# Split weights written at 32 different word offsets in their buffers, in a two-layer hybrid decoder trunk

## The chip, the cores and the metric

One core of one Trainium2 chip runs one program. The metric is the device time of one execution in microseconds; the kernel before was timed at 1593.85 us, the median of two runs (1593.66 and 1594.04).

## The reference

The kernel computes a small decoder trunk in float32: 256 tokens of width 1024 pass through two layers, each with a half-step SwiGLU feed-forward (width 2816), a mixing sub-layer with two branches (a Mamba-2 state-space branch and a gated DeltaNet branch on the same normalised input), and a second feed-forward; a last RMS norm closes it.

```python
for l in range(DEPTH):
    h = h + 0.5 * swiglu(rms_norm(h, ffn1_norm[l]), ffn1_w_in[l], ffn1_w_out[l])
    u = rms_norm(h, mix_norm[l])
    (z_s, xbc, dt_s, qkv, z_d, b_d, a_d, gate_s, gate_d) = jnp.split(u @ w_in[l], split_points, axis=-1)
    y_s = mamba2_branch(z_s, xbc, dt_s, ...)
    y_d = deltanet_branch(qkv, z_d, b_d, a_d, ...)
    merged = (jax.nn.sigmoid(gate_s) * (y_s @ ssm_w_branch[l])
              + jax.nn.sigmoid(gate_d) * (y_d @ dn_w_branch[l]))
    h = h + merged @ w_out[l]
    h = h + 0.5 * swiglu(rms_norm(h, ffn2_norm[l]), ffn2_w_in[l], ffn2_w_out[l])
return rms_norm(h, final_norm)
```

Nearly all of the arithmetic is in the products with the large weight matrices: w_in and w_out of the four feed-forwards, w_in of the mixer, the two branch projections and the mixer's w_out.

## The kernel before

The weights are laid out on the host, by pure reordering, as one stream of units of 128 x 2048 float32, in the order in which the kernel consumes them. A unit is used in two halves of 128 x 1024 words; there are 504 half units in all, numbered j.

Each half unit passes three stations. `load(j)` (line 93) issues a DMA on SyncE's queue into one of five `wraw` buffers. `prep(j)` (line 98) splits it: ScalarE copies the raw weights into `whi`, whose type is float32r and so rounds them, and VectorE subtracts, `wlo = wraw - whi`. `whi` and `wlo` have five buffers each. `take()` (line 111) hands the pair to the next consumer; each call also runs the loads and the splits ahead, so that up to five pairs stand ready and four more raw halves are on their way. Before the change every `whi` and `wlo` buffer is a tile of 128 x 1024 and is written from its first word.

The activations are split in the same way into a high and a low part. A product is then three float32r matmuls that add into one PSUM bank: high by high, and the two cross terms. Two helpers issue them: `mm3` (lines 208 to 211) with the weights as the streamed operand, 512 columns at a time, and the activations as the stationary one; `mm3w` (lines 213 to 216) with 128 columns of the weights as the stationary operand and 256 tokens of `uTh` or `uTl` streamed.

Three routines consume the half units. `tok_chunk` (line 218) is for outputs with tokens on the partitions: four half units, `mm3`, stationary `uTh` and `uTl`; its results are the tiles named f and t. `chan_chunk` (line 235) is for outputs with channels on the partitions: two half units, `mm3w`; its results are fc in the feed-forwards, and kk, qq, vv, zd, bc and xs in the mixer. `out_chunks` (line 254) is for the down projections: one half unit per 128 input channels, `mm3`, stationary `gh` and `gl` in the feed-forwards, `bh` and `bl` in the branch projections, `mh` and `ml` in the mixer's output; its results are named o and b. One further product, psm, uses `mm3w` with a small weight tile of 48 columns (`wsh`, `wsl`) that is split separately.

In a profile, a matmul is printed as output, then the streamed tile, then the stationary one: "fc<-uTh,whi" streams uTh against stationary whi, and "o<-whi,gh" streams whi against stationary gh. TensorE's weight loads stand in rows of their own under PEld.

The order of instructions on each engine follows the program, with a few pieces moved up by priority or held back behind a named instruction; the mixer's steps follow a list written out by hand (`ORDER`, lines 38 to 42). The tiles are placed in the on-chip memory by pools in the order of their creation: `h`, the constants, `uTh` and `uTl` and the norm weights first, then the five `wraw`, the five `whi` and the five `wlo` buffers, and behind them the large slots (`gh`, `gl` and the mixer's tiles), the 512-word scratch tiles (`bh`, `bl` and others) and the small ones. In the program as built, all five `whi` and all five `wlo` buffers lie 4096 bytes apart and begin on a multiple of 64 bytes within the partition; `uTh` and `uTl` begin 32 bytes past such a multiple; `gh`, `gl`, `bh`, `bl`, `mh`, `ml`, `wsh` and `wsl` on one.

Of the kernel before, what the change touches and what calls it, by code (L numbers as in the profile page):

```python
# [8 lines left out]
F32R = mybir.dt.float32r  # L9
I32 = mybir.dt.int32  # L10
AF = mybir.ActivationFunctionType
ALU = mybir.AluOpType
# [4 lines left out]
P = 128  # L17
# [12 lines left out]
NRAW = 5  # L30
NSPL = 5
START = 2

# [10 lines left out]
def trunk_kernel(ctx, tc, x, wst, wsm, norms, lpar, rpar, cst, out):  # L46
# [4 lines left out]
    wpool = ctx.enter_context(tc.tile_pool(name="wpool", bufs=1))  # L51
# [7 lines left out]
    def act(o, i, func=AF.Copy, **kw):  # L59
        return A.activation(out=o, in_=i, func=func, **kw)  # L60

    def tt(o, a, b, op):
        return V.tensor_tensor(out=o, in0=a, in1=b, op=op)  # L63
# [9 lines left out]
    def f(ap):  # L73
        return ap.bitcast(F32)
# [22 lines left out]

    def prep(j):
        r = raws.pop(j)
        hi = wpool.tile([P, 1024], F32R, tag="whi", name="whi", bufs=NSPL)  # L100
        lo = wpool.tile([P, 1024], F32R, tag="wlo", name="wlo", bufs=NSPL)
        act(hi[:], r[:])
        tt(lo[:], r[:], f(hi[:]), ALU.subtract)
        halves[j] = (hi, lo)

    def ahead(key, n, fn):
        while state[key] < min(n, n_halves):
            fn(state[key])
            state[key] += 1

    def take():
        j = state["taken"]
        state["taken"] = j + 1
        ahead("loaded", j + NSPL + NRAW - 1, load)
        ahead("prepped", j + 1 if state["hold"] else j + NSPL, prep)
        return halves.pop(j)
# [46 lines left out]
    def rstd_of(t):  # L163

        ss = small([P, 2], "ss")
        for n in range(2):
            junk = tmp2("junk")
            act(junk[:], h[:, t, n * 512 : (n + 1) * 512], AF.Square, scale=1.0 / 32.0, accum_out=ss[:, n : n + 1])
        z = small([P, 2], "zz")
        ts(z[:, 0:1], ss[:, 0:1], ss[:, 1:2], ALU.add, EPS, ALU.add)  # L170
        rsqrt(z[:, 1:2], z[:, 0:1], [P, 1])
        return z[:, 1:2]
# [18 lines left out]
    def norm_in(nw, add=None):  # L191

        for t in range(2):
            with tc.high_priority(offset=PRI):
                if add:
                    add(t)
                ins, done = rms_chain(t, nw)
            if t == 0:
                state["hold"] = False
                n = state["taken"]  # L200
                if not add:
                    ahead("prepped", n + 1, prep)
                    with tc.issue_after(done[0].ins), tc.issue_after(done[1].ins):
                        ahead("prepped", n + START, prep)
                with tc.issue_after(ins.ins):
                    ahead("prepped", n + 2, prep)
# [813 lines left out]
    for t in range(2):  # L1020
# [5 lines left out]
        r = rstd_of(t)  # L1026
# [123 lines left out]
```

## Time and profile before

| | us |
|---|---|
| Median of the two timed runs | 1593.85 |
| The profiled execution, its own time | 1593.43 |
| Span of its trace, first to last instruction | 1591.6 |
| DMA of one raw half unit (512 KB), issue to landing | 4.3 |
| ScalarE waiting before whi, all causes | 429.3 |
| VectorE waiting before wlo, all causes | 376.4 |

The mean granted TensorE clock is 0.999 of full speed over the span. A row of the profile's groups gives a line of the kernel, the engine, the operation and its tiles, then the total busy time, the mean of one instruction in nanoseconds, and the idle time of the engine just before. In rows of instructions in order of time, the first number is the start and the second the duration, both in microseconds. Matmuls overlap: each row's duration runs from entry to the modelled end of its pipeline, so that consecutive rows cover each other, and the pace of TensorE is the distance from start to start.

### The profile page before, as it was taken

What the parts mean: (1) busy time and instruction counts of PE and PEld (TensorE: products, weight loads), DVE (VectorE), ACT (ScalarE), POOL (GpSimd) and SP (SyncE); (2) the same over time, 40 slices, a digit from 0 to 9 for tenths busy, and PEclk for the clock granted to TensorE, in tenths of its full rate; (3) what the DMA queues carried; (4) which work ended last, traced back from release to release, by engine and by line L of the source; (5) the groups of instructions that cost most, each with busy time, mean ns of one, the idle gap of its engine ahead of it and who ended that gap; (6) DMA issues with size and microseconds to landing.
All of it is one profiled execution on the core that took longest, in us unless ns stands there. A gap on an engine that the chain in (4) does not pass through costs nothing.

```text
span 1591.6 us, 28859 instructions
## 1 busy us (share of the span) xinstructions
PE 1572.3 (99%) x11672; PEld 1420.9 (89%) x11672; DVE 1069.1 (67%) x1550; ACT 880.1 (55%) x1416; POOL 58.1 (4%) x60
## 2 busy tenths in 40 slices
PE   8999999999999999999999999999999999999998
PEld 7999879999888888999899987899998888889986
DVE  5555468957899766555465555698579996675554
ACT  5444468756565654444354444686656665454443
POOL 0000020000000000000000001000000000000000
PEclk9999999999999999999999999999999999999999
DMA  7555465543465456555565565655436555555562
GB/s 268 193 188 195 161 203 192 166 149 117 173 214 172 159 170 189 188 192 190 173 207 190 186 196 174 197 176 180 129 120 207 178 170 175 172 175 194 187 196 96
DMA packets 91915, 284.73 MB, mean 179 GB/s; under 512 B 22069, under 2 KB 23045, under 8 KB 90758
## 3 DMA queue, kind: packets, MB, share of 16 engines
q1 hardware_dynamic: 91782, 282.90, 54.8%
q8 instruction: 91, 1.49, 0.4%
q14 instruction: 42, 0.34, 0.1%
HBM read 280.94 MB, written 1.92 MB: 178 GB/s over the span
## 4 chain that ended last, share of the span: by engine, by line
PE 91%; DVE 4%; DMA 2%; ACT 1%; POOL 1%; issue 0%; SPq 0%; POOLq 0%; ACTq 0%
PE fc L216 9%; PE fc L214 9%; PE fc L215 9%; PE o L211 6%; PE o L209 5%; PE o L210 5%; PE t L209 4%; PE t L210 3%; PE t L211 3%; PE b L211 3%; PE b L210 2%; PE b L209 2%; PE xs L215 2%; PE xs L214 2%; PE xs L216 2%; DVE wlo L63 1%
## 5 line engine op out<-in xcount | busy, mean ns | idle before, releaser
L63 DVE TENSOR_TENSOR wlo<-wraw,whi 128x1024 fp32r<-128x1024 f32 x504 | 613.6, 1223 | 376.4 <-ACT whi L60 369.3
L60 ACT ACTIVATE whi<-wraw 128x1024 fp32r<-128x1024 f32 x504 | 531.0, 1060 | 429.3 <-PE fc L215 176.2
L214 PE MATMUL fc<-uTh,whi 128*128 128x256 f32 x1280 | 357.4, 279 | 0.0
L215 PE MATMUL fc<-uTl,whi 128*128 128x256 f32 x1280 | 357.0, 279 | 0.0
L216 PE MATMUL fc<-uTh,wlo 128*128 128x256 f32 x1280 | 357.0, 279 | 0.0
L215 PEld LDWEIGHTS fc<-uTl,whi 128*128 128x128 f32 x1280 | 240.6, 188 | 0.2
L214 PEld LDWEIGHTS fc<-uTh,whi 128*128 128x128 f32 x1280 | 240.6, 188 | 0.2
L216 PEld LDWEIGHTS fc<-uTh,wlo 128*128 128x128 f32 x1280 | 240.6, 188 | 0.0
L209 PE MATMUL o<-whi,gh 128*128 128x512 f32 x352 | 137.3, 390 | 0.0
L210 PE MATMUL o<-wlo,gh 128*128 128x512 f32 x352 | 137.3, 390 | 0.0
L211 PE MATMUL o<-whi,gl 128*128 128x512 f32 x352 | 137.0, 389 | 0.0
L209 PE MATMUL t<-whi,uTh 128*128 128x512 f32 x256 | 103.2, 404 | 1.0 <-ACT uTh L60 1.0
L210 PE MATMUL t<-wlo,uTh 128*128 128x512 f32 x256 | 101.6, 397 | 0.0
L211 PE MATMUL t<-whi,uTl 128*128 128x512 f32 x256 | 101.1, 396 | 0.0
L211 PEld LDWEIGHTS o<-whi,gl 128*128 128x128 f32 x352 | 66.1, 188 | 13.8
L210 PEld LDWEIGHTS o<-wlo,gh 128*128 128x128 f32 x352 | 66.1, 188 | 13.6
L209 PEld LDWEIGHTS o<-whi,gh 128*128 128x128 f32 x352 | 66.1, 188 | 13.4
L209 PE MATMUL b<-whi,bh 128*128 128x512 f32 x192 | 76.3, 399 | 0.0
L210 PE MATMUL b<-wlo,bh 128*128 128x512 f32 x192 | 74.9, 390 | 0.0
L211 PE MATMUL b<-whi,bl 128*128 128x512 f32 x192 | 74.3, 394 | 0.6 <-DVE bl L63 0.6
L214 PE MATMUL xs<-uTh,whi 128*128 128x256 f32 x256 | 73.1, 286 | 0.0
L216 PE MATMUL xs<-uTh,wlo 128*128 128x256 f32 x256 | 71.6, 280 | 0.0
(259 smaller groups left out, 2915.6 us busy)
## 6 DMA issues: line engine op xcount, KB each, us to landing
wraw<-in_wst_dram SPq DMA_DIRECT2D x504, 512.0 KB, 4.3
dc<-rdram SPq DMA_DIRECT2D x8, 1024.0 KB, 9.2
nw<-in_norms_dram SPq DMA_DIRECT2D x6, 512.0 KB, 4.9
gb<-rdram SPq DMA_DIRECT2D x8, 256.0 KB, 6.1
h<-in_x_dram SPq DMA_DIRECT2D x4, 256.0 KB, 3.1
out_dram<-fo SPq DMA_DIRECT2D x4, 256.0 KB, 2.3
dq<-X SPq DMA_DIRECT2D x2, 256.0 KB, 4.8
cs<-in_cst_dram SPq DMA_DIRECT2D x1, 384.0 KB, 8.2
```

Of the source, the lines that this page charges most:

```text
L60: return A.activation(out=o, in_=i, func=func, **kw)
L63: return V.tensor_tensor(out=o, in0=a, in1=b, op=op)
L209: PE.matmul(ps, lh, rh, start=start, stop=False)
L210: PE.matmul(ps, lh, rl, start=False, stop=False)
L211: PE.matmul(ps, ll, rh, start=False, stop=stop)
L214: PE.matmul(ps, wh, mh, start=start, stop=False)
L215: PE.matmul(ps, wh, ml, start=False, stop=False)
L216: PE.matmul(ps, wl, mh, start=False, stop=stop)
```

## The change

One constant is added and `prep` is changed. Every `whi` and `wlo` buffer gets 32 words per partition more, and half unit j is written at words j mod 32 to j mod 32 + 1023 of its buffer instead of 0 to 1023. The views of those 1,024 words are what `take()` hands out, so the consumers read the weights at the same offset. The raw buffers, the loads, the number and the order of instructions on every engine, and the arithmetic are as before. All tiles that are placed behind the buffers move up by 1,280 bytes (ten buffers, 128 bytes each).

```diff
 START = 2
+STEPS = 32
...
     def prep(j):
         r = raws.pop(j)
-        hi = wpool.tile([P, 1024], F32R, tag="whi", name="whi", bufs=NSPL)
-        lo = wpool.tile([P, 1024], F32R, tag="wlo", name="wlo", bufs=NSPL)
-        act(hi[:], r[:])
-        tt(lo[:], r[:], f(hi[:]), ALU.subtract)
+        at = slice(j % STEPS, j % STEPS + 1024)
+        hi = wpool.tile([P, 1024 + STEPS], F32R, tag="whi", name="whi", bufs=NSPL)[:, at]
+        lo = wpool.tile([P, 1024 + STEPS], F32R, tag="wlo", name="wlo", bufs=NSPL)[:, at]
+        act(hi, r[:])
+        tt(lo, r[:], f(hi), ALU.subtract)
         halves[j] = (hi, lo)
```

## The prediction

> **What bounds the kernel now.** I read the busy shares and the chain of waits first, then the groups of matmuls, then the starts of single matmuls in order of time.
>
> ```profile
> span 1591.6 us, 28859 instructions
> ...
> PE 1572.3 (99%) x11672; PEld 1420.9 (89%) x11672; DVE 1069.1 (67%) x1550; ACT 880.1 (55%) x1416; POOL 58.1 (4%) x60
> ...
> PE 91%; DVE 4%; DMA 2%; ACT 1%; POOL 1%; issue 0%; SPq 0%; POOLq 0%; ACTq 0%
> ...
> L63 DVE TENSOR_TENSOR wlo<-wraw,whi 128x1024 fp32r<-128x1024 f32 x504 | 613.6, 1223 | 376.4 <-ACT whi L60 369.3
> L60 ACT ACTIVATE whi<-wraw 128x1024 fp32r<-128x1024 f32 x504 | 531.0, 1060 | 429.3 <-PE fc L215 176.2
> ```
>
> TensorE is busy for 1572.3 of 1591.6 us and is 91% of the chain. The two instructions whose addresses change most directly, the rounding on ScalarE and the subtraction on VectorE, wait for others (429.3 and 376.4 us): they have room. So the time is the number of matmuls times the interval between their starts, and the question is whether that interval depends on where an operand begins.
>
> ```profile
> L214 PE MATMUL fc<-uTh,whi 128*128 128x256 f32 x1280 | 357.4, 279 | 0.0
> L214 PE MATMUL xs<-uTh,whi 128*128 128x256 f32 x256 | 73.1, 286 | 0.0
> L214 PE MATMUL zd<-uTh,whi 128*128 128x256 f32 x128 | 36.3, 284 | 0.0
> L214 PE MATMUL bc<-uTh,whi 128*128 128x256 f32 x128 | 36.3, 283 | 0.1
> L214 PE MATMUL qq<-uTh,whi 128*128 128x256 f32 x128 | 36.1, 282 | 0.0
> L214 PE MATMUL vv<-uTh,whi 128*128 128x256 f32 x128 | 35.9, 281 | 0.0
> L214 PE MATMUL kk<-uTh,whi 128*128 128x256 f32 x128 | 35.9, 281 | 0.0
> ...
> L209 PE MATMUL o<-whi,gh 128*128 128x512 f32 x352 | 137.3, 390 | 0.0
> L209 PE MATMUL t<-whi,uTh 128*128 128x512 f32 x256 | 103.2, 404 | 1.0 <-ACT uTh L60 1.0
> L209 PE MATMUL b<-whi,bh 128*128 128x512 f32 x192 | 76.3, 399 | 0.0
> L209 PE MATMUL f<-whi,uTh 128*128 128x512 f32 x64 | 26.5, 416 | 1.3 <-ACT uTh L60 1.3
> L209 PE MATMUL o<-whi,mh 128*128 128x512 f32 x64 | 25.1, 393 | 0.0
> ```
>
> Each of these rows stands for three (L214 to L216, or L209 to L211). The upper seven, 3 x (1280 + 256 + 5 x 128) = 6,528 matmuls, load the split weights as the stationary operand (named last) and stream 256 columns of uTh or uTl. The lower five, 3 x (352 + 256 + 192 + 64 + 64) = 2,784 matmuls, stream 512 columns of the split weights. The durations in these rows overlap, since matmuls are pipelined; what counts is start to start:
>
> ```profile
> 1529.72 0.39 PE L209 MATMUL o<-whi,gh 128*128 128x512 f32 x1
> ...
> 1543.32 0.39 PE L209 MATMUL o<-whi,gh 128*128 128x512 f32 x1
> ...
> 448.01 0.40 PE L209 MATMUL t<-whi,uTh 128*128 128x512 f32 x1
> ...
> 458.97 0.40 PE L211 MATMUL t<-whi,uTl 128*128 128x512 f32 x1
> ...
> 1499.85 0.28 PE L215 MATMUL fc<-uTl,whi 128*128 128x256 f32 x1
> ...
> 1511.75 0.28 PE L215 MATMUL fc<-uTl,whi 128*128 128x256 f32 x1
> ...
> 218.22 0.28 PE L214 MATMUL psm<-uTh,wsh 128*48 128x256 f32 x1
> ...
> 221.01 0.40 PE L209 MATMUL t<-whi,uTh 128*128 128x512 f32 x1
> ```
>
> These are the first and last of stretches without a gap: o 60 intervals in 13.60 us, 226.7 ns each; t 47 in 10.96, 233.2; fc 102 in 11.90, 116.7; psm 24 in 2.79, 116.3. The rows show that o and t, the same shape with the same streamed tile, differ by 6.5 ns, and twice 116.7 is 233.3. What differs by the program's own placement is the start of an operand: whi, wlo, gh, gl, wsh and wsl begin on multiples of 64 bytes in their partition, uTh and uTl 32 bytes (8 words) past one. Where no operand is off a 64-byte boundary (o), 512 columns take 226.7; where the stationary one is off (t), 233.2; where the streamed one is off (fc, psm), 256 columns take 116.7, which is 3.3 more than half of 226.7. This is the only evidence on alignment in the trace, and I rest the forecast on it.
>
> **The change part by part.** No instruction, transfer, wait or queue position is added, removed or moved. Ten buffers grow by 128 bytes each, which moves later tiles by 1,280 bytes, 20 x 64, so that gh, gl, bh and the rest stay on their 64-byte boundaries; uTh and uTl lie ahead of the buffers and stay put. What changes is that 30 of every 32 half units begin off a 64-byte boundary, 7.5 words on average past one.
>
> Stationary side, 6,528 matmuls. Price: the 6.5 ns of t over o, for 8 words past a boundary. Whether each word costs 0.81 ns (7.5 x 0.81 = 6.1), or any offset costs the whole step (15/16 x 6.5 = 6.1), the mean is 6.1 ns: 6,528 x 6.1 = 39.8 us. Bounds: nothing at all (the load is hidden, below), and for a load at half its speed
>
> ```profile
> L214 PEld LDWEIGHTS fc<-uTh,whi 128*128 128x128 f32 x1280 | 240.6, 188 | 0.2
> L214 PEld LDWEIGHTS psm<-uTh,wsh 128*48 128x48 f32 x16 | 1.9, 121 | 0.1
> ```
>
> (188 - 121) / 80 = 0.84 ns per column, so 107 ns more for 128 columns. I take the value of t against o, since it is the same kind of instruction.
>
> Streamed side, 2,784 matmuls. Price: 116.7 - 226.7 / 2 = 3.3 ns for 8 words, 3.1 on average: 2,784 x 3.1 = 8.6 us. Bounds: nothing, and the slowest that such a matmul ever ran here, at the start of the program:
>
> ```profile
> 12.79 0.63 PE L210 MATMUL f<-wlo,uTh 128*128 128x512 f32 x1
> 13.22 0.63 PE L211 MATMUL f<-whi,uTl 128*128 128x512 f32 x1
> 13.64 0.63 PE L209 MATMUL f<-whi,uTh 128*128 128x512 f32 x1
> ```
>
> 425 ns apart, about 197 over the 228 that I take as the mix of o and t. On both sides the lower bound reaches below nothing too: TensorE's interval is not proved to be the best one, and a new relation of the two operands could shorten it.
>
> [...]
>
> Writes, 504 on ScalarE and 504 on VectorE (which also reads whi at the new offset). The convolution already reads and writes ca at words 1, 2 and 3:
>
> ```profile
> L66 DVE SCALAR_TENSOR_TENSOR ca<-xs,lp,ca 128x255 f32<-128x255 f32 x32 | 15.2, 477 | 1.9 <-ACT ca L60 1.9
> L66 DVE SCALAR_TENSOR_TENSOR ca<-xs,lp,ca 128x254 f32<-128x254 f32 x32 | 15.0, 474 | 0.1
> L66 DVE SCALAR_TENSOR_TENSOR ca<-xs,lp,ca 128x253 f32<-128x253 f32 x32 | 15.0, 473 | 0.1
> ...
> 475.00:590.00 115.00, 114.70 (x686) 95.23 (x684) 90.14 (x119) 66.36 (x95) 4.50 (x3) 1.00 0.51 169
> ```
>
> The 477, 474 and 473 ns follow the element count; an odd first word (255, 253) costs nothing to see. ScalarE shows no such write. I take both at zero. If each write took a quarter longer (0.25 x 613.6 = 153 us on VectorE), the cover would be VectorE's idle time: even in its fullest stretch, the branch stage from 475 to 590 us, it is busy 90 of 115 us and has some 40 of the 504 writes, 12 us more.
>
> Sum: 39.8 + 8.6 = 48 us on TensorE, all of it on the chain, since nothing on TensorE waits for other work there. Profiled execution: its span 1591.6 us, its own time 1593.43, against a median of 1593.85 (0.4 above). 1593.85 + 48 = 1642, plus 3%.
>
> **The rivals.** (A) The lower-cost one, on the other side: not slower. The next weights load while the matmul before runs. In fc the columns of a load need 128 x 0.84 = 107 ns of the 116.7, which leaves 9.6 ns, more than the 6.1 of the stationary side. psm speaks for it: its load is 67 ns shorter, and its interval is the same, so the load's length does not bind. Against it: t has 126 ns of room for its load and yet pays 6.5. If the load's extra is hidden and only the streamed side pays, at most what o loses against t: 8.6 us, or (3 x (352 + 64 + 192)) x 6.5 = 11.9 us. About 1604, within 2%. It decides if the fc interval stays at 116.7.
>
> (B) Odd words break something coarser. In the trace of before every streamed or stationary operand with split weights begins on an even word, so nothing there shows what an odd one does. Half of the new offsets are odd. At the 425 ns above for half of the streamed matmuls: 1,392 x 197 = 274 us, 1,868 in all. If odd loads take 107 ns more too, less the 9.6 of room, 3,264 x 97 = 317 us come on top, 2,185. For it: one word in 128 columns may not be fetched like 8 words; against it: the convolution's rows above, on another engine. [...]
>
> (C) Faster. By the present placement all buffers begin at the same place modulo 4,096 bytes. If the early 425 ns are twice an undisturbed interval, which is an estimate and no more, 256 undisturbed columns take 425 / 4 = 106.3, and the 10.4 ns up to 116.7 would be collisions between the two operands; staggering could take half of that: 6,528 x 5.2 = 34 us, 1,560. Against: the same interval in every stretch and for all five buffers, and t, the one staggered case, is the slower one.
>
> (D) The offset never reaches the instructions: the time stays 1,594. Every reader takes its slices from the stored pair, so hardly.
>
> **How the numbers follow.** About 2% (32 us: 1,562 to 1,626) is what a measurement of this kernel can tell from no change. The forecast, 1,642, has 0.40; A 0.22; B 0.30; C 0.06; D 0.02. C is faster; A and D, and 0.01 of the forecast (the part in which its 48 us come out under 32), are within 2%; the rest is slower: 0.06, 0.25, 0.69. The range runs from 1,592, below A and D, to 1,868, the first price of B; left out are C and the part of B in which the loads pay too (0.12).
>
> **What would show it.** In the profile after: fc intervals near 122.8 and o near 229.8 or above prove the two terms; fc at 116.7 proves A; intervals that jump between neighbouring half units, by odd and even, prove B. The counts must stay the same, the rows of whi and wlo at 1060 and 1223 ns. The forecast is wrong if TensorE begins to wait for ScalarE or VectorE, which would mean that the writes pay.

## The result and the profile after

The changed kernel takes 1613.54 us (median of two runs, 1612.12 and 1614.96) against 1593.85: a ratio of 1.0124, 95% interval 1.008 to 1.0167. It is 19.7 us slower: less than the 2% that the prediction set as its bound, but the whole interval lies above 1. The profiled execution took 1614.96 us, with a span of 1613.2.

The page of the changed kernel (busy shares, chain, groups; its lines from `prep` on are one or two numbers higher than before):

```profile
span 1613.2 us, 28859 instructions
...
PE 1592.3 (99%) x11672; PEld 1433.9 (89%) x11672; DVE 1070.3 (66%) x1550; ACT 882.5 (55%) x1416; POOL 58.0 (4%) x60
...
PE 91%; DVE 3%; DMA 2%; ACT 1%; POOL 1%; issue 0%; SPq 0%; POOLq 0%; ACTq 0%
...
L64 DVE TENSOR_TENSOR wlo<-wraw,whi 128x1024 fp32r<-128x1024 f32 x504 | 614.4, 1224 | 391.2 <-ACT whi L61 388.6
L61 ACT ACTIVATE whi<-wraw 128x1024 fp32r<-128x1024 f32 x504 | 532.8, 1061 | 455.0 <-PE fc L217 182.1
L216 PE MATMUL fc<-uTh,whi 128*128 128x256 f32 x1280 | 359.7, 281 | 0.0
...
L217 PEld LDWEIGHTS fc<-uTl,whi 128*128 128x128 f32 x1280 | 241.0, 188 | 0.2
...
L211 PE MATMUL o<-whi,gh 128*128 128x512 f32 x352 | 139.3, 396 | 0.0
```

The counts are the same, and TensorE is again 91% of the chain. The two writes take 1061 and 1224 ns, as before (1060 and 1223), and ScalarE and VectorE wait longer than before: the time is TensorE's own, 20 us more of it, in the same number of matmuls. The mean duration of a row says little here, since rows overlap (the row of o<-whi,gh has a mean of 396 ns, and o's matmuls start 232.7 ns apart); a count of matmuls in a stretch of fixed length says more. These are busy times in two stretches of the first feed-forward, its channel products (40 to 130 us) and its down projection (145 to 185 us): after the stretch and its length come TensorE's busy time with the number of matmuls in brackets, then its weight loads, VectorE, ScalarE, GpSimd, the granted clock, the busy share of the DMA engines and the GB/s that they moved. Before:

```profile
40.00:130.00 90.00, 90.00 (x773) 90.00 (x773) 50.34 (x57) 43.46 (x57) 0.00 (x0) 1.00 0.59 190
145.00:185.00 40.00, 40.00 (x178) 33.12 (x177) 17.71 (x15) 15.88 (x15) 0.00 (x0) 1.00 0.62 198
```

and after:

```profile
40.00:130.00 90.00, 90.00 (x764) 90.00 (x763) 49.87 (x56) 42.80 (x56) 0.00 (x0) 1.00 0.56 185
145.00:185.00 40.00, 40.00 (x173) 32.42 (x172) 17.89 (x16) 15.24 (x15) 0.00 (x0) 1.00 0.58 190
```

TensorE is busy throughout at the full clock in both, and gets through 764 matmuls in place of 773, and 173 in place of 178. Over the whole trace, the mean distance from one start to the next (distances that hold a pause are left out: those above 140 ns for the channel products, above 250 for the others) is:

| ns from start to start | before | after | number | us more |
|---|---|---|---|---|
| channel products (weights stationary) | 116.7 | 118.3 | 6,528 | 10.4 |
| o (weights streamed) | 227.1 | 232.7 | 1,248 | 7.0 |
| b (weights streamed) | 228.2 | 232.8 | 576 | 2.6 |
| t and f (weights streamed) | 233.2 | 232.8 | 960 | -0.4 |

The last column is number times difference; it sums to 19.6 of the 21.6 us by which the spans of the two traces differ (1591.6 and 1613.2). So nearly all of the result is pace.

Inside the changed kernel the pace follows the first word. Rows of TensorE in order of time: the first matmul of each of four turns of one channel product, which takes two half units in turn (words 24, 25, 24, 25), and of each of four successive half units of the down projection (words 17, 18, 19 and 20):

```profile
81.77 0.28 PE L216 MATMUL fc<-uTh,whi 128*128 128x256 f32 x1
...
83.14 0.28 PE L216 MATMUL fc<-uTh,whi 128*128 128x256 f32 x1
...
84.56 0.28 PE L216 MATMUL fc<-uTh,whi 128*128 128x256 f32 x1
...
85.92 0.28 PE L216 MATMUL fc<-uTh,whi 128*128 128x256 f32 x1
...
152.37 0.40 PE L211 MATMUL o<-whi,gh 128*128 128x512 f32 x1
...
155.20 0.39 PE L211 MATMUL o<-whi,gh 128*128 128x512 f32 x1
...
158.03 0.39 PE L211 MATMUL o<-whi,gh 128*128 128x512 f32 x1
...
160.77 0.39 PE L211 MATMUL o<-whi,gh 128*128 128x512 f32 x1
```

Each step is 12 matmuls. At words 17 and 18, 2.83 / 12 = 235.8 ns; at word 19, 2.74 / 12 = 228.3. In the channel product, 1.37 and 1.36 us at word 24 are 114.2 and 113.3 ns, faster than the 116.7 of before; 1.42 at word 25 is 118.3. So the offset acts, and it acts on both sides. It doesn't act by distance from a boundary: word 24 is half way between two multiples of 64 bytes, and faster than word 0 was before.

### The profile page after: what moved, and what is told of

The parts are those of the page before. It is cut to its first block, busy times and chain, and to the rows that moved or that the text cites. A ratio compares the mean times of both kernels' runs of the same rounds, so it can differ in the third digit from the quotient of the medians.

```text
span 1613.2 us, 28859 instructions
## 1 busy us (share of the span) xinstructions
PE 1592.3 (99%) x11672; PEld 1433.9 (89%) x11672; DVE 1070.3 (66%) x1550; ACT 882.5 (55%) x1416; POOL 58.0 (4%) x60
## 4 chain that ended last, share of the span: by engine, by line
PE 91%; DVE 3%; DMA 2%; ACT 1%; POOL 1%; issue 0%; SPq 0%; POOLq 0%; ACTq 0%
PE fc L218 9%; PE fc L217 9%; PE fc L216 9%; PE o L213 6%; PE o L211 6%; PE o L212 6%; PE t L211 4%; PE t L212 3%; PE t L213 3%; PE b L213 3%; PE b L212 2%; PE b L211 2%; PE xs L217 2%; PE xs L216 2%; PE xs L218 2%; DVE wlo L64 1%
## 5 line engine op out<-in xcount | busy, mean ns | idle before, releaser
L64 DVE TENSOR_TENSOR wlo<-wraw,whi 128x1024 fp32r<-128x1024 f32 x504 | 614.4, 1224 | 391.2 <-ACT whi L61 388.6
L61 ACT ACTIVATE whi<-wraw 128x1024 fp32r<-128x1024 f32 x504 | 532.8, 1061 | 455.0 <-PE fc L217 182.1
```

## The experiments

Ratios are to the kernel before, run on the same chip, with 95% intervals. The intervals from start to start are means over the whole trace, formed as in the table above.

### The larger buffers without the offset, and constant offsets

In the changed kernel the word is made constant, 0, 8 or 1:

```diff
-        at = slice(j % STEPS, j % STEPS + 1024)
+        w = 0        # then 8, then 1
+        at = slice(w, w + 1024)
```

> The larger buffers (1,056 words) are kept, but every half unit is written from word 0. Theory 'starts' (only the first word of the operands matters): the time of before, 1594 us, with o at 226.7 ns from start to start and fc at 116.7. Rival 'placement' (the buffers' new spacing of 4,224 bytes, or the tiles moved up by 1,280 bytes, cost the time): 1614 us, like the changed kernel.

1.0102 (1.0085 to 1.0118), 1611.58 us. This is near the 1614 of the rival 'placement': with every half unit at word 0 of its buffer, as before, most of the change's extra time is there. The two stretches of this kernel:

```profile
40.00:130.00 90.00, 90.00 (x758) 90.00 (x757) 48.76 (x56) 42.14 (x55) 0.00 (x0) 1.00 0.57 188
145.00:185.00 40.00, 40.00 (x174) 32.48 (x174) 18.42 (x16) 15.90 (x15) 0.00 (x0) 1.00 0.59 196
```

758 matmuls in the channel stretch are fewer than with the turning offsets. Channel products 118.6 ns, o 231.0, b 230.6, t 233.1.

> Every half unit at word 8 (32 bytes). Theory 'boundary' (the prediction's: each operand pays by how far past a 64-byte boundary it starts): channel matmuls 116.7 + 6.5 = 123.2 ns, streamed ones 3.3 more, 1594 + 42 + 9 = 1645 us. Theory 'settled' (some pairs of starts let TensorE fall into a faster even pace, 226.7 or 113.3, all others run near 233 and 117 to 119): o and b go from 227 to about 233 (+11 us), channel matmuls to the 118.8 that they show at word 8 in the changed kernel (+14 us), about 1618 us.

1.0126 (1.0111 to 1.0141), 1615.67 us; channel products 118.8, o 232.8, b 232.3, t 231.4. 'Boundary' (1645) is out by 30 us; 'settled' (1618) fits, in the intervals too. Against word 0 of the same buffers, word 8 adds 4 us, and 0.2 ns to the channel products.

> Every half unit at word 1. 'Boundary', by words: one eighth of the cost at word 8, 1600 us; as a step for any offset: 1645 us. 'Settled' with a share of the place within 16 bytes: o, b and t at 236.5 ns as at words 1, 5, 9 of the changed kernel (+17 and +3 us), channel matmuls at 118.7 (+13 us), about 1627 us.

1.0168 (1.0151 to 1.0185), 1622.36 us; channel products 118.5, o 235.4, b 234.9, t 236.9. Nearest is 'settled' (1627), and word 1 is worse than word 8 for the streamed side. All three runs hold the placement's cost too, as the first showed.

### Moving uTh and uTl, with the larger buffers

```diff
-    uTh = cpool.tile([P, KT, S], F32R, name="uTh")
+    uTh = cpool.tile([P, KT * S + 32], F32R, name="uTh")[:, 24 : 24 + KT * S]
+    uTh = uTh.rearrange("p (k t) -> p k t", k=KT)
...
-        at = slice(j % STEPS, j % STEPS + 1024)
+        w = 0
+        at = slice(w, w + 1024)
```

The same is done for uTl, which so also stands 128 bytes further behind uTh; the weight buffers move by 256 bytes.

> Half units at word 0 and uTh and uTl moved by 96 bytes, so that all operands of the split products start on a multiple of 128 bytes. 'Boundary': t falls from 233.2 to 226.7 ns (960 of them, 6 us), channel matmuls from 116.7 to 113.3 (6,528, 22 us): 1566 us. 'Settled', if the relation of the two starts is what counts: the same 1566 us. Rival 'the tile' (t and fc are slower than o by the shape of their loops, not by their addresses): 1594 us.

1.0076 (1.006 to 1.0092), 1607.76 us: against the first experiment, which is the one to compare with, 4 us less, where 28 were expected. Channel products 118.0, t 231.7. None of the three fits. With the placement's cost in it, and uTl parted from uTh, this run couldn't decide.

### Which part of the placement costs

Three things in the placement changed at once: the later tiles moved by 1,280 bytes, the five buffers no longer stand 4,096 bytes apart, and lo no longer stands a multiple of 4,096 bytes behind hi (the distance is 5 x 4,224 = 21,120). The first of these alone, in the kernel before:

```diff
         lo = wpool.tile([P, 1024], F32R, tag="wlo", name="wlo", bufs=NSPL)
+        if j == 0:
+            wpool.tile([P, 320], F32, tag="gap", name="gap")
```

> The buffers of before (4,096 bytes apart, written from word 0); behind them lies an unused gap of 1,280 bytes, so that only the later tiles (gh, gl, bh, bl and so on) stand where the change puts them. Theory 'pair' (what costs is that whi and wlo of one half unit no longer begin a multiple of 4,096 bytes apart): 1594 us. Rival 'later tiles' (the relation of the weights to gh, gl, bh, bl changed): o and b at 231 instead of 227 ns, fc unchanged at 116.7: 1594 + 1,824 x 3.5 ns = 1600 us.

1.0006 (0.9995 to 1.0016): no cost. Channel products 116.7, o 227.0.

Hi and lo in one buffer, 4,096 bytes apart, with w = 0 and then w = j % 32:

```diff
-        hi = wpool.tile([P, 1024], F32R, tag="whi", name="whi", bufs=NSPL)
-        lo = wpool.tile([P, 1024], F32R, tag="wlo", name="wlo", bufs=NSPL)
+        w = 0        # then j % 32
+        both = wpool.tile([P, 2112], F32R, tag="whl", name="whl", bufs=NSPL)
+        hi, lo = both[:, w : w + 1024], both[:, w + 1024 : w + 2048]
...
```

> hi and lo halves in one buffer of 2,112 words, lo exactly 4,096 bytes behind hi, from word 0; the five buffers stand 8,448 bytes apart and the later tiles where the change puts them. Theory 'pair': fc back at 116.7 and o at 227 ns, 1594 us. Rival 'spacing' (the five buffers must stand a multiple of 4,096 bytes apart): as with the larger buffers written from word 0, 1611 us. Rival 'later tiles': 1600 us.

1.0007 (0.9998 to 1.0017): the placement's cost is gone with the pair put right, the later tiles where the change has them. The buffers, 8,448 = 33 x 256 bytes apart, also all begin at the same place modulo 256 bytes again, as before; with a spacing of 4,224 this place alternates from buffer to buffer.

```profile
40.00:130.00 90.00, 90.00 (x774) 90.00 (x773) 49.59 (x57) 42.95 (x56) 0.00 (x0) 1.00 0.60 189
145.00:185.00 40.00, 40.00 (x178) 33.15 (x177) 17.87 (x15) 15.71 (x15) 0.00 (x0) 1.00 0.63 198
```

> As the run before, but each half unit written at word j mod 32 of this buffer, lo still 4,096 bytes behind hi: the change's offsets with the pair kept together. If the offsets alone cost little: o, b and t between 230 and 236 ns by the place of the first word within 16 bytes, mean 233 (+10 us on o and b), channel matmuls near 116.7, about 1604 us. If the offsets cost what the prediction said: 1642 us. If hi and lo 4,096 apart are of no matter: 1614 us, as the changed kernel.

1.0101 (1.0083 to 1.012), 1612.22 us. The offsets alone cost as much as the larger buffers alone (1.0102), and both together (the change) not twice as much: 1.0124. Channel products 118.0, o 232.7, b 232.5, t 232.8. The expectation of 1604 had taken the channel products as unmoved; they moved by 1.3 ns.

### How far apart hi and lo may stand

The kernel before, with an unused gap between the five whi and the five wlo buffers:

```diff
         hi = wpool.tile([P, 1024], F32R, tag="whi", name="whi", bufs=NSPL)
+        if j == 0:
+            wpool.tile([P, 32], F32, tag="gap", name="gap")     # then 64, 128, 256 words
         lo = wpool.tile([P, 1024], F32R, tag="wlo", name="wlo", bufs=NSPL)
```

> The buffers of before, written from word 0, with one unused gap of 128 bytes between the five whi and the five wlo buffers, so that lo stands a multiple of 4,096 bytes plus 128 behind hi. If 128 bytes already part the pair: 1611 us, as in the larger buffers (where the distance is 128 past a multiple of 512). If only a larger part of the address counts: 1594 us.

1.0101 (1.0077 to 1.0125), 1612.33 us, from one gap of 128 bytes. It moves wlo and the tiles behind it, gh, gl, bh, bl, mh and ml among them; whi, uTh and uTl stay. The channel products read none of the tiles behind, and go from 116.7 to 118.8 ns: 6,528 x 2.1 = 14 of the 16.6 us by the medians come from wlo's new place. By steps, the distance from a whi matmul to the next whi matmul goes from 116.7 to 117.2, from whi to wlo from 116.9 to 118.3, and from wlo to whi from 116.6 to 121.0. On the streamed side (o 229.0, b 229.6) the moved stationary tiles may have a share.

> As the run before with a gap of 256 bytes. Back at 1594 us if the pair only has to agree modulo 256 bytes; 1605 us or more if the span is wider.

0.9993 (0.9983 to 1.0003): no cost.

> Gap of 512 bytes. 1594 us if the pair has to agree modulo 512 bytes or less; 1605 us or more if wider.

0.9996 (0.9986 to 1.0005): none.

> Gap of 1,024 bytes. 1594 us if the pair has to agree modulo 1,024 bytes or less; 1605 us or more if up to 4,096 bytes count.

1.0002 (0.9993 to 1.0012): none. The channel stretch with the gaps of 128 and of 256 bytes:

```profile
40.00:130.00 90.00, 90.00 (x759) 90.00 (x759) 48.70 (x56) 43.26 (x56) 0.00 (x0) 1.00 0.58 186
```

```profile
40.00:130.00 90.00, 90.00 (x774) 90.00 (x773) 50.45 (x57) 43.37 (x56) 0.00 (x0) 1.00 0.60 189
```

Of the four gaps, those of 256, 512 and 1,024 bytes leave the pace alone, and the one of 128 costs 1%. The change's 21,120 bytes are 82 x 256 + 128. What the runs don't separate is whether the distance between whi and wlo counts or the place of each of them modulo 256 bytes against uTh and uTl: every run that parts the pair also changes the place of one of the two, or of both, against uTh, and every run without a cost leaves all tiles at their places modulo 256.

### Moving uTh and uTl, with the buffers of before

The kernel before, with uTh and uTl in one tile, both moved by 96 bytes. The tile is 128 bytes longer, so the weight buffers and all tiles behind move by 128 bytes, and against the weights uTh and uTl move by 32 bytes, onto a multiple of 256:

```diff
+    uT = cpool.tile([P, 2 * KT * S + 32], F32R, name="uT")
+    uTh, uTl = (
+        uT[:, 24 + i * KT * S : 24 + (i + 1) * KT * S].rearrange("p (k t) -> p k t", k=KT) for i in range(2)
+    )
```

> The weights of before; uTh and uTl moved by 96 bytes to a multiple of 128, still 8,192 bytes apart from each other. If o owes its 226.7 ns to operands that all start on such multiples, and t and fc only lack that: t 226.7 (-6 us), channel matmuls 113.3 (-22 us), 1566 us. If what counts is hi against lo of the weights alone: 1594 us.

1.0103 (1.0087 to 1.0119), 1612.25 us. Half of the expectation came true: t and f fell from 233.2 to 227.6 ns, the pace of o. The channel products did the opposite:

```profile
40.00:130.00 90.00, 90.00 (x752) 90.00 (x751) 48.54 (x55) 42.46 (x55) 0.00 (x0) 1.00 0.58 184
```

752 in place of 773, and 119.9 ns over the trace in place of 116.7. With all operands of the split products at the same place modulo 256 bytes, the streamed weights run at the pace that o had before and the stationary ones at the slowest mean of any kernel run here.

### Each side alone, a boundary, and a better word

The pair kept together, and w by the consumer of half unit j (`USE` is a string with "c" for channel products, "t" for token products and "o" for down projections, in the order of the stream). Each run has one of these four lines, and they are reported in this order:

```diff
+        w = j % 32 if USE[j] == "c" else 0      # stationary alone
+        w = 0 if USE[j] == "c" else j % 32      # streamed alone
+        w = 16
+        w = 0 if USE[j] == "o" else 27
```

> lo 4,096 bytes behind hi; the turning offsets only for half units that serve as the stationary operand (the channel products), word 0 for the others. By the intervals: channel matmuls at 118.0 instead of 116.7 ns, 6,528 x 1.3 = 8 us: 1602 us. By the prediction's stationary term: 1634 us.

1.004 (1.0026 to 1.0053), 1603.13 us: near the 1602 that the intervals gave, and not the 1634 of the prediction's term. Channel products 118.1, o 227.1.

> lo 4,096 bytes behind hi; the turning offsets only for half units that are streamed, word 0 for the channel products. By the intervals: o 227 to 232.7, b 228.1 to 232.4, t unchanged: 1,248 x 5.7 + 576 x 4.3 = 9.6 us, 1603 us. By the prediction's streamed term: the same, 1602 us, but with t slower too.

1.0047 (1.0031 to 1.0062), 1604.49 us; o 232.7, b 232.5, t and f 232.9. The two sides' extra, 0.40% and 0.47%, sum to about the 1.01% of both, within the intervals.

> lo 4,096 bytes behind hi; every half unit at word 16, a multiple of 64 bytes. 'Boundary' (the prediction's cost of a start off a 64-byte multiple): no cost, 1594 us. By the intervals by word: o 230, b 231 and t 231, channel matmuls 118.2 ns: 6,528 x 1.5 + 1,824 x 3 - 960 x 2 = about 13 us, 1607 us.

1.0079 (1.0062 to 1.0095), 1609.48 us. A start on a multiple of 64 bytes isn't free: the channel products, at 118.3, pay as much as the mean of the turning offsets. The intervals' 1607 is near, but o 229.0 and b 229.4 came out lower and t 233.3 higher than expected.

> lo 4,096 bytes behind hi; half units for the channel and the token products at word 27, those for the down projections at word 0. From the intervals by word of the turning offsets with the pair kept together: channel matmuls 113.6 instead of 116.7 ns (6,528 x 3.1 = 20 us), t at 228.9 instead of 233.2 (960 x 4.3 = 4 us), o and b as before: 1570 us, a gain. If such intervals only hold while neighbouring half units differ: 1594 us or slower.

0.9862 (0.9846 to 0.9878), 1574.56 us: faster than both kernels. Its stretches and shares:

```profile
span 1572.6 us, 28767 instructions
...
PE 1548.3 (98%) x11672; PEld 1400.7 (89%) x11672; DVE 1063.4 (68%) x1550; ACT 879.6 (56%) x1416; POOL 60.4 (4%) x60
```

```profile
40.00:130.00 90.00, 90.00 (x797) 90.00 (x796) 51.10 (x59) 45.63 (x59) 0.00 (x0) 1.00 0.60 193
145.00:185.00 40.00, 40.00 (x178) 33.13 (x177) 17.85 (x15) 15.38 (x16) 0.00 (x0) 1.00 0.64 197
```

797 matmuls in the channel stretch in place of 773. Channel products 113.5 ns (116.7 before), t and f 229.8 (233.2), o as before: 6,528 x 3.2 + 960 x 3.4 = 24 us by the intervals. The medians of this set, 1596.98 before and 1574.56, differ by 22.

## Why the prediction was right or wrong

What bounds the kernel, and that every nanosecond in a matmul's interval lands on the time: right. The four terms of the table hold no wait, and sum to 19.6 of the 21.6 us between the traces.

The writes, taken at zero: right (1061 against 1060 ns, 1224 against 1223).

The streamed term, 8.6 us from 2,784 matmuls: its size was right (9.2 us in the table, and a ratio of 1.0047 with the streamed side alone), but not its reason, so that the agreement is luck. It was to be a cost per word past a 64-byte boundary, on every stretch. In fact t paid nothing, and o and b lost the 227 ns that they alone had. What the runs show is that o's pace is a special case: turning offsets put all three at 232.5 to 232.9.

The stationary term, 39.8 us, is where the sum failed: it was 10.4 (118.3 ns per matmul in place of the 122.8 that it needed). The step was to price the stationary side by "the 6.5 ns of t over o, for 8 words past a boundary". That difference is real and does come from uTh's start against the weights, since t fell to 227.6 when only the places of the tiles were changed. But it isn't a price per word that another loop would pay as well. Channel products at word 8 ran at 118.8 with the pair parted, not at 123.2, and those at word 0 of the same buffers at 118.6; at word 16, on a boundary, they still pay 1.6 ns; at word 27 they gain 3.2; and with uTh on a boundary, the case that the prediction's reading calls free, they run at 119.9. The starts of the operands together set the pace, not the distance of either from a boundary.

"Ten buffers grow by 128 bytes each" was followed only to the later tiles, which indeed cost nothing (1.0006). The step missed where whi and wlo stand: the same growth turns their distance from a multiple of 4,096 into 128 past a multiple of 256, and lets each buffer's place modulo 256 alternate. Moving wlo and what lies behind it by 128 bytes costs 1.0101, the larger buffers alone 1.0102, and the offsets with the pair kept together 1.0101. So the loss has two causes, the larger buffers and the offsets, and either alone brings most of it.

The rivals. The result lies within 2%, the outcome to which the prediction gave 0.25. A, "hidden", gave 1604 by leaving the channel products at 116.7; they moved to 118.3, so it was near for a wrong reason. B, odd words: no halving at any word. Over o, b and t of the changed kernel, words 0, 1, 2 and 3 past a multiple of 4 run at 231.7, 236.3, 232.9 and 230.0 ns, and with the pair kept together at 231.5, 235.8, 233.5 and 229.8: one odd place is the slowest and the other the fastest. This repeats every 16 bytes: in the changed kernel each of the eight words one past a multiple of 4 runs at 235.3 to 236.7 ns, and each of the other 24 at 229.9 to 234.0. But the place within 16 bytes isn't all: the channel products at the words three past a multiple of 4 go from 114.9 ns (word 27) to 119.9 (word 15), and the pair counts too (1.0101 with a gap of 128 bytes). C, collisions that another relation of the operands would avoid, was right that there is time to gain (0.9862 with word 27) and wrong that turning the offsets would find it: few of the 32 words are good for the channel products. In the changed kernel only words 21, 24 and 27 lie below the 116.7 ns of before (116.3, 114.7 and 114.9), and with the pair kept together they run at 114.4 at word 21 and 113.4 at word 27, with means of 118.3 and 118.0 over all words. That collisions are the reason isn't shown. The 425 ns of B and C come back in the middle of the changed kernel: six intervals of t from 428.42 to 430.98 us take 427 ns each, at a granted clock of 0.50, and eleven from 431.24 to 433.78 take 231, at 1.00. So there the pace went with the clock; that half of it is an undisturbed interval, C's estimate, isn't shown. D is out: the pace follows the first word.

Not settled is what happens in the memory or in TensorE that makes a move by 128 bytes matter (1.0101) and one by 256 not (0.9993), the first word's place within 16 bytes matter (230.0 to 236.3 ns for o, b and t), and words such as 27 good for the channel products (113.5); nor whether it is the distance between whi and wlo that counts or the place of each against uTh and uTl.

## What to carry to other kernels

Where matmuls follow each other without a gap, print the distance from start to start by operand addresses before and after any change of buffer sizes: here padding alone cost 1%, with the same counts and the same time for each write. A difference between two loops is a price only for a change that turns one loop into the other; before it is carried over to a third loop, measure that loop at two or three constant offsets. An experiment that keeps the buffers of the change and takes away only what it meant to do separates the aim from the side effect, and belongs first.

## What the runs showed of the hardware that was not expected

- Streams of float32r matmuls without a gap hold different paces by address alone, at a mean granted clock of 0.996 of full speed or more in every trace: 113.5 to 119.9 ns for 256 columns, 227 to 236.9 for 512.
- Where two tiles that take turns as operands (whi, whi, wlo) stand counts: 256, 512 and 1,024 bytes more between them cost nothing (0.9993, 0.9996, 1.0002), 128 bytes more cost 1.0101, 16.6 us by the medians.
- Moving uTh and uTl by 32 bytes against the weights sped one product up by 5.6 ns per matmul (t and f, to 227.6) and slowed another down by 3.2 (the channel products, to 119.9).
